# Making h of layer 0 in five turns of 2, 3, 3, 4 and 4 d-tiles, with the adaLN sums of all but the first on VectorE

## The chip, the cores and the metric

The kernel runs on one core of one Trainium2 chip. The metric is the device time of one execution in microseconds; lower is better. Of the kernel before there are three runs, and one further execution that was profiled.

## What is computed

Two layers of a hybrid block over x (256 frames, 2048 channels, float32). The part that matters here is the head of a layer, the conditioned norm (adaLN) and the large input projection:

```python
mod = c_act @ ada_w + ada_b                      # (1, 2048) @ (2048, 6144)
shift, scale, res_gate = jnp.split(mod, 3, axis=-1)
h = rms_norm(x, norm_pre) * (1.0 + scale[:, None, :]) + shift[:, None, :]
proj = h @ w_in                                  # (256, 2048) @ (2048, 14400)
```

Three mixers (retention, a gated recurrence, latent attention) work on slices of `proj`; their outputs are projected, merged by gates, projected again, normed and added to x. Shift and scale of a layer need 2 x 2048 x 2048 weights of `ada_w`, 32 MB, for one row of activations.

## The kernel before

Activations are held with the channels on the 128 partitions, in tiles of 128 channels ("d-tiles"; a layer has 16, `NKT`). Every float32 product is made from split operands: a weight tile is loaded, ScalarE casts it to `wh` (the high part) and VectorE computes `wl = raw - wh` (the rest); then TensorE does three products, xh wh, xh wl, xl wh.

**Loads and splits.** `load_raw` (line 307) issues every load of weights and of adaLN rows on SP, into a ring of four buffers of 1 MB (`rawp`). `load_split` (L331, L332) casts and subtracts in pieces of 1024 columns, into rings of three buffers each (`whp`, `wlp`). A weight tile is 1024 output columns by two d-tiles, 1 MB, in two pieces. The instruction `recent` is the subtraction of the newest tile's first piece.

**Order.** TensorE and SP run in the order in which the code issues their instructions. ScalarE, VectorE and GpSimd are ordered by the framework from priorities (splits 400, closing of sums 300) and dependences; `tc.issue_after(i)` says that what follows comes no earlier than i.

**Turns of layer 0.** Layer 0 starts while no h exists. `KBLOCKS` cuts the 16 d-tiles of h into four blocks of 4. For every block a turn runs over seven groups of 1024 columns of `w_in` (`first`: lx, lg, mqkv, mg, two groups of logits, rq), each with the d-tiles of this block alone: two weight tiles a group, 14 a turn. A group's four PSUM banks (of six in all) are closed after each turn: the first turn's partial sums are copied to SBUF by ScalarE (L473), later ones are added there by VectorE (L475, four adds of 128 x 512 a group). Groups lx, lg, mg and rq hold the weights stationary (`gemm_w`, L416 to L418, 256 columns), the other three the activations (`gemm_x`, L398, 512 columns). In `gemm_x` the steps of the last weight tile of a turn are sorted by halves of the frames.

**The next block, step by step.** While a turn runs, the next block of h is made by a generator, `h_block`. `keep_pace` is called once in each weight tile (in the middle of a tile of two d-tiles) and takes as many steps of the generator as its share of the turn asks: 13 steps (`turns`) over 14 tiles. A step of `ada_strips` loads `nr` rows of `ada_w` per partition (`ada_load`: 512 columns, 4 rows, 1 MB); four loads make the sum for the shift, four that for the scale.

**Two ways to sum.** A sum over 2048 rows has 16 rows on each partition. *Strips*: TensorE multiplies each row (L573) by a matrix of 32 columns, `c_strip`, whose first holds the activation, into one of four strips of 32 partitions of a bank; four strips run side by side. *Adds*: VectorE multiplies a row by the activation and adds it to an accumulator (`ada_add`, L523 for the first, L525 for the others; `issue_after(recent)`), one step after the load. `ON_VECTOR` says which loads go to VectorE: none in the first block, three of four in the others; then eight closing products with `one_strip` (L579) bring the accumulator into the strips' bank. ScalarE copies the bank (L580), TensorE transposes it (L584), VectorE sums over the strips (L587). After both sums `gains` makes the two per-channel factors, and `h_tiles` transposes one or two d-tiles of the normed x (L685), scales them and splits them (L690 or L692, L700, L701).

**Start-up.** The first block has nothing beside it: x, eight adaLN loads and the first weight tiles come in this order, at high priority; half the block's steps go ahead of the first weight load (`early`). Its four d-tiles are scaled on VectorE (L692), later blocks' on ScalarE (L690).

Of the kernel before, what the change touches and what calls it, by code (L numbers as in the profile page):

```python
# [19 lines left out]
P = 128  # L20
# [8 lines left out]
KBLOCKS = [(0, 4), (4, 8), (8, 12), (12, 16)]  # L29
ON_VECTOR = [(), (0, 1, 2), (0, 1, 2), (0, 1, 2)]  # L30
# [25 lines left out]
def hybrid_trunk(ctx: ExitStack, tc: tile.TileContext, a, out):  # L56
# [59 lines left out]
    def mbank():  # L116
        return pm.tile([P, 512], F32, tag="mi", name=nm("mi"))
# [4 lines left out]
    def v3(t, b):  # L122
        return t.rearrange("p (a b) -> p a b", b=b)
# [79 lines left out]
    one_strip = cpool.tile([P, P], F32, name="one_strip")[:, 0:STRIP]  # L203
    nc.gpsimd.memset(one_strip, 0.0)
    nc.gpsimd.memset(one_strip[:, 0:1], 1.0)
# [338 lines left out]
    def ada_strips(l, k0, k1, on_vector):  # L544
# [7 lines left out]
        for which, c0 in enumerate((k0 * P, D + k0 * P)):  # L552
            acc, b = half_slot(ncol), None
            waiting, adds, strips = None, 0, 0

            def add():
                with ExitStack() as order:
                    if recent:
                        order.enter_context(tc.issue_after(recent[-1]))
                    ada_add(acc, waiting, adds == 0)  # L560

            for i, r0 in enumerate(range(0, NKT, nr)):
                rows = ada_load(l, c0, ncol, r0)
                if waiting is not None:
                    add()
                    waiting, adds = None, adds + 1
                if i in on_vector:
                    waiting = rows
                else:
                    b = mbank() if b is None else b  # L570
                    for r, src in rows:
                        j = r % 4 * STRIP
                        mm(b[j:j + STRIP, 0:ncol], c_strip[:, r, :], src, start=strips < 4, stop=not on_vector and r >= NKT - 4, skip_group_check=True)  # L573
                        strips += 1
                yield 1
            if on_vector:
                for i in range(n):
                    j, cs = i * STRIP, slice(i * P, (i + 1) * P)
                    mm(b[j:j + STRIP, cs], one_strip, acc[:, cs], start=False, stop=True, skip_group_check=True)  # L579
            nc.scalar.copy(acc, b[:, 0:ncol])  # L580
# [5 lines left out]
            sums = b[:, 0:ncol].rearrange("p (i j s) -> p i j s", j=4, s=STRIP)[:, :, :, 0]  # L586
# [833 lines left out]
```

## Time and profile before

| | us |
|---|---|
| median of 3 runs (lowest, highest) | 1977.23 (1972.63, 1978.14) |
| profiled execution: its time, its span | 1970.52, 1968.8 |
| PE (TensorE) busy | 1913.3 (97%) |
| VectorE (DVE) busy | 1374.1 (70%) |
| ScalarE (ACT) busy | 963.9 (49%) |
| split's casts, L331 / rests, L332 | 662.3 / 791.4 |

Times in rows are microseconds from the start of the span, busy times are unions of spans, and a mean is in nanoseconds where it says so. PE is TensorE, PEld its weight loads, DVE VectorE, ACT ScalarE, POOL GpSimd, SP the engine that issues the loads. Matmuls overlap, so the distance between starts tells more than a duration. "Idle before" is the time that the engine stood still ahead of an instruction, and behind the arrow stands what ended it.

### The profile page before, as it was taken

What the parts mean: (1) busy time and instruction counts of PE and PEld (TensorE: products, weight loads), DVE (VectorE), ACT (ScalarE), POOL (GpSimd) and SP (SyncE); (2) the same over time, 40 slices, a digit from 0 to 9 for tenths busy, and PEclk for the clock granted to TensorE, in tenths of its full rate; (3) what the DMA queues carried; (4) which work ended last, traced back from release to release, by engine and by line L of the source; (5) the groups of instructions that cost most, each with busy time, mean ns of one, the idle gap of its engine ahead of it and who ended that gap; (6) DMA issues with size and microseconds to landing.
All of it is one profiled execution on the core that took longest, in us unless ns stands there. A gap on an engine that the chain in (4) does not pass through costs nothing.

```text
span 1968.8 us, 25569 instructions
## 1 busy us (share of the span) xinstructions
PE 1913.3 (97%) x10172; PEld 1624.4 (83%) x10172; DVE 1374.1 (70%) x1761; ACT 963.9 (49%) x1252; POOL 104.6 (5%) x89
## 2 busy tenths in 40 slices
PE   4999999989999999999989999999999999999998
PEld 1987989878888888888879888888898888888886
DVE  3668778898877677878766765446675447887565
ACT  3553436934544445444454775444455444544443
POOL 0000000100000010102010010000000001010100
PEclk9999999999999999999999999999999999999999
DMA  9868685468776788888855555555554656877663
GB/s 327 295 219 313 248 304 183 142 234 287 250 268 239 265 271 272 286 284 275 292 205 192 171 171 194 193 190 182 187 185 153 203 192 216 277 283 282 214 214 128
DMA packets 163192, 457.09 MB, mean 232 GB/s; under 512 B 12224, under 2 KB 12240, under 8 KB 163072
## 3 DMA queue, kind: packets, MB, share of 16 engines
q1 hardware_dynamic: 159392, 443.44, 65.4%
q0 software_dynamic: 3536, 11.75, 2.1%
q8 instruction: 79, 1.29, 0.3%
q14 instruction: 41, 0.34, 0.0%
q10 hardware_dynamic: 144, 0.26, 0.0%
HBM read 451.23 MB, written 4.19 MB: 231 GB/s over the span
## 4 chain that ended last, share of the span: by engine, by line
PE 86%; DVE 7%; DMA 4%; ACT 2%; issue 1%; SPq 0%; DVEq 0%; ACTq 0%
PE acc L398 57%; PE acc L432 7%; PE acc L433 4%; PE acc L418 3%; PE acc L417 3%; PE acc L416 3%; DVE wl L332 3%; DMA raw<-in_w_in 2%; DVE slot L525 1%; DMA raw<-in_ada_w 1%; ACT wh L331 1%; PE mi L1003 1%; PE mi L852 1%; PE mi L851 1%; PE mi L573 0%
## 5 line engine op out<-in xcount | busy, mean ns | idle before, releaser
L332 DVE TENSOR_TENSOR wl<-raw,wh 128x1024 fp32r<-128x1024 f32 (+1 forms) x636 | 791.4, 1248 | 488.3 <-ACT wh L331 486.0
L331 ACT CAST wh<-raw 128x1024 fp32r<-128x1024 f32 (+1 forms) x636 | 662.3, 1045 | 826.9 <-PE acc L398 450.4
L398 PE MATMUL acc<-wh,pair 128*128 128x512 f32 x3552 | 991.5, 393 | 2.5 <-ACT wh L331 2.5
L398 PEld LDWEIGHTS acc<-wh,pair 128*128 128x128 f32 x3552 | 660.9, 188 | 146.8 <-issue 9.3
L398 PE MATMUL acc<-wl,pair 128*128 128x512 f32 x1776 | 558.0, 390 | 3.1 <-DVE wl L332 3.1
L398 PEld LDWEIGHTS acc<-wl,pair 128*128 128x128 f32 x1776 | 332.7, 188 | 76.4 <-DVE wl L332 6.6
L525 DVE SCALAR_TENSOR_TENSOR slot<-raw,c_act,slot 128x512 f32<-128x512 f32 x306 | 230.8, 755 | 5.0
L432 PE MATMUL acc<-pair,wh 128*128 128x512 f32 x640 | 228.9, 401 | 0.0
L416 PE MATMUL acc<-pair,wh 128*128 128x256 f32 x640 | 183.3, 286 | 2.4 <-ACT pair L700 1.1
L433 PE MATMUL acc<-pair,wl 128*128 128x256 f32 x640 | 180.5, 282 | 2.7 <-DVE wl L332 2.7
L418 PE MATMUL acc<-pair,wl 128*128 128x256 f32 x640 | 181.5, 284 | 1.4 <-DVE wl L332 1.4
L417 PE MATMUL acc<-pair,wh 128*128 128x256 f32 x640 | 181.4, 283 | 0.5 <-DVE pair L701 0.5
L432 PEld LDWEIGHTS acc<-pair,wh 128*128 128x128 f32 x640 | 120.9, 189 | 28.9
L416 PEld LDWEIGHTS acc<-pair,wh 128*128 128x128 f32 x640 | 123.1, 192 | 3.5 <-ACT pair L700 1.6
L433 PEld LDWEIGHTS acc<-pair,wl 128*128 128x128 f32 x640 | 121.7, 190 | 3.5 <-DVE wl L332 3.3
L418 PEld LDWEIGHTS acc<-pair,wl 128*128 128x128 f32 x640 | 123.0, 192 | 1.8 <-DVE wl L332 1.8
L417 PEld LDWEIGHTS acc<-pair,wh 128*128 128x128 f32 x640 | 123.1, 192 | 1.0 <-DVE pair L701 0.7
L1202 POOL TENSOR_TENSOR slot<-slot,slot 128x512 f32<-128x512 f32 x32 | 51.5, 1625 | 319.5 <-DVE slot L1199 319.5
L475 DVE TENSOR_TENSOR slot<-acc,slot 128x512 f32<-128x512 f32 x84 | 54.0, 685 | 5.6 <-PE acc L418 4.0
L573 PE MATMUL mi<-raw,c_strip 128*32 128x512 f32 x112 | 21.7, 865 | 21.9 <-DMA raw<-in_ada_w 21.9
L1199 DVE TENSOR_TENSOR slot<-acc,slot 128x512 f32<-128x512 f32 x48 | 31.9, 683 | 2.2 <-PE acc L398 2.1
L479 ACT ACTIVATE slot<-acc 128x512 f32<-128x512 f32 x48 | 27.3, 596 | 9.7 <-PE acc L398 8.9
(250 smaller groups left out, 1300.8 us busy)
## 6 DMA issues: line engine op xcount, KB each, us to landing
raw<-in_w_in SPq DMA_DIRECT2D x224, 1024.0 KB, 5.0
raw<-in_ada_w SPq DMA_DIRECT2D x96, 1024.0 KB, 6.8
raw<-in_w_branch SPq DMA_DIRECT2D x48, 1024.0 KB, 6.4
raw<-in_w_out SPq DMA_DIRECT2D x32, 1024.0 KB, 5.5
raw<-in_mla_w_ukv SPq DMA_DIRECT2D x8, 1024.0 KB, 6.4
raw<-in_mla_w_uq SPq DMA_DIRECT2D x8, 768.0 KB, 4.5
slot<-in_x SPq DMA_DIRECT2D x8, 512.0 KB, 8.7
slot<-in_k_decay POOLq DMA_DIRECT2D x4, 512.0 KB, 4.5
```

Source lines behind the costliest of these rows:

```text
L331: nc.scalar.copy(wh, raw[:, c0:c0 + n])
L332: sub = nc.vector.tensor_tensor(out=wl, in0=raw[:, c0:c0 + n], in1=wh.bitcast(F32), op=ALU.subtract)
L398: mm(b[:, 0:w_n], x, ws[:, j * w_n:(j + 1) * w_n], start=st, stop=sp)
L416: mm(dst, wh[:, cs], act.H(kt), start=first, stop=False, skip_group_check=True)
L417: mm(dst, wh[:, cs], act.L(kt), start=False, stop=False, skip_group_check=True)
L418: mm(dst, wl[:, cs], act.H(kt), start=False, stop=last, skip_group_check=True)
L432: mm(v3(b, T), wh[:, cs], act.both(kt), start=kt == 0, stop=False)
L433: mm(b[:, 0:T], wl[:, cs], act.H(kt), start=False, stop=kt == NKT - 1)
L475: nc.vector.tensor_tensor(out=dst, in0=b, in1=dst, op=ALU.add)
L525: nc.vector.scalar_tensor_tensor(acc, src, ada_scalar(r), acc, ALU.mult, ALU.add)
L1199: nc.vector.tensor_tensor(out=gate[hf][:, cs], in0=banks[hf][j], in1=gate[hf][:, cs], op=ALU.mult)
L1202: nc.gpsimd.tensor_tensor(out=dst, in0=dst, in1=gate[hf][:, cs], op=ALU.add)
```

## The change

- `KBLOCKS` is 2, 3, 3, 4 and 4 d-tiles: five turns instead of four. In turns of three d-tiles each group has a weight tile of two d-tiles (1 MB) and one of one (512 KB); the first turn has one tile a group.
- Only the first block is summed by strips. It has 256 columns: two loads of 8 rows a sum, in pieces of 1 KB. `one_strip` and its closing products are gone.
- In all other blocks every load goes to VectorE: 16 adds a sum, of 384 columns in the second and third block (4 rows a load, 768 KB) and of 512 in the fourth and fifth. A load's adds come one step after it, behind the newest tile's first rest. There is no closing product and no copy: the accumulator is transposed as it is and summed over all 128 columns that it then has (the partitions before).
- The pace follows by its formula: 13 steps over 7 tiles in the first turn, 13 over 14 in the others.
- d-tiles from 2 on (before: from 4 on) are scaled on ScalarE, by the condition on `KBLOCKS[1][0]`.

```diff
--- before.py
+++ after.py
@@ -26,8 +26,7 @@
 ROPE = 64
 EPS = 1e-6
 W1 = 1024
-KBLOCKS = [(0, 4), (4, 8), (8, 12), (12, 16)]
-ON_VECTOR = [(), (0, 1, 2), (0, 1, 2), (0, 1, 2)]
+KBLOCKS = [(0, 2), (2, 5), (5, 8), (8, 12), (12, 16)]
 STRIP = 32
 LATE = 800
 ASIDE = [((0, 3),), ((0, 3), (1, 0))]
@@ -200,9 +199,6 @@
     c_strip = cpool.tile([P, NKT, STRIP], F32, name="c_strip")
     nc.gpsimd.memset(c_strip, 0.0)
     nc.vector.tensor_copy(c_strip[:, :, 0], c_act)
-    one_strip = cpool.tile([P, P], F32, name="one_strip")[:, 0:STRIP]
-    nc.gpsimd.memset(one_strip, 0.0)
-    nc.gpsimd.memset(one_strip[:, 0:1], 1.0)
 
     x0 = a["x"].rearrange("b (h p) d -> h p (b d)", p=P)
     out_v = out.rearrange("b (h p) d -> h p (b d)", p=P)
@@ -541,7 +537,7 @@
             use(i, acc)
             release(acc)
 
-    def ada_strips(l, k0, k1, on_vector):
+    def ada_cols(l, k0, k1, strips):
 
 
 
@@ -550,40 +546,33 @@
         nr = 1 << int(math.log2(2048 // ncol))
         cols = small([P, 8], "adac", 2)[:, 0:2 * n]
         for which, c0 in enumerate((k0 * P, D + k0 * P)):
-            acc, b = half_slot(ncol), None
-            waiting, adds, strips = None, 0, 0
-
-            def add():
-                with ExitStack() as order:
-                    if recent:
-                        order.enter_context(tc.issue_after(recent[-1]))
-                    ada_add(acc, waiting, adds == 0)
-
-            for i, r0 in enumerate(range(0, NKT, nr)):
-                rows = ada_load(l, c0, ncol, r0)
-                if waiting is not None:
-                    add()
-                    waiting, adds = None, adds + 1
-                if i in on_vector:
+            acc = half_slot(ncol)
+            if strips:
+                b = mbank()
+                for r0 in range(0, NKT, nr):
+                    for r, src in ada_load(l, c0, ncol, r0):
+                        j = r % 4 * STRIP
+                        mm(b[j:j + STRIP, 0:ncol], c_strip[:, r, :], src, start=r < 4, stop=r >= NKT - 4, skip_group_check=True)
+                    yield 1
+                nc.scalar.copy(acc, b[:, 0:ncol])
+            else:
+                waiting = None
+                for r0 in range(0, NKT + nr, nr):
+                    rows = ada_load(l, c0, ncol, r0) if r0 < NKT else None
+                    if waiting is not None:
+                        with tc.issue_after(recent[-1]):
+                            ada_add(acc, waiting, r0 == nr)
                     waiting = rows
-                else:
-                    b = mbank() if b is None else b
-                    for r, src in rows:
-                        j = r % 4 * STRIP
-                        mm(b[j:j + STRIP, 0:ncol], c_strip[:, r, :], src, start=strips < 4, stop=not on_vector and r >= NKT - 4, skip_group_check=True)
-                        strips += 1
-                yield 1
-            if on_vector:
-                for i in range(n):
-                    j, cs = i * STRIP, slice(i * P, (i + 1) * P)
-                    mm(b[j:j + STRIP, cs], one_strip, acc[:, cs], start=False, stop=True, skip_group_check=True)
-            nc.scalar.copy(acc, b[:, 0:ncol])
+                    if r0 < NKT:
+                        yield 1
             yield 1
             b = mbank()
             for i in range(n):
                 nc.tensor.transpose(b[:, i * P:(i + 1) * P], acc[:, i * P:(i + 1) * P], ident)
             release(acc)
-            sums = b[:, 0:ncol].rearrange("p (i j s) -> p i j s", j=4, s=STRIP)[:, :, :, 0]
+            sums = v3(b[:, 0:ncol], P)
+            if strips:
+                sums = b[:, 0:ncol].rearrange("p (i j s) -> p i j s", j=4, s=STRIP)[:, :, :, 0]
             nc.vector.reduce_sum(out=cols[:, which * n:(which + 1) * n], in_=sums, axis=AX.X)
         gains(l, cols[:, n:2 * n], cols[:, 0:n], k0, k1)
         yield 1
@@ -1105,13 +1094,13 @@
         macc = [[None, None] for _ in range(2)]
         freed = set()
 
-        def h_block(k0, k1, on_vector):
+        def h_block(k0, k1, strips):
             c0 = k0 * P
             while c0 < k1 * P:
                 c1 = min(k1 * P, (c0 // W1 + 1) * W1)
                 normed(xs, xs, r, c0, c1)
                 c0 = c1
-            yield from ada_strips(0, k0, k1, on_vector)
+            yield from ada_cols(0, k0, k1, strips)
             k = k0
             while k < k1:
                 n = 1 if k % 2 else min(2, k1 - k)
@@ -1126,7 +1115,7 @@
                 k0, k1 = KBLOCKS[bi]
                 return 2 * (NKT // (1 << int(math.log2(16 // (k1 - k0)))) + 1) + 1 + (k1 - k0 + 1) // 2
 
-            h0 = start("h0", h_block(*KBLOCKS[0], ON_VECTOR[0]))
+            h0 = start("h0", h_block(*KBLOCKS[0], True))
             last = len(KBLOCKS) - 1
             with tc.high_priority(offset=LATE):
                 for _ in range(turns(0) // 2 + 1):
@@ -1138,7 +1127,7 @@
                 if bi == last:
                     release(*xs[0], *xs[1])
                 else:
-                    ahead = start(f"h{bi + 1}", h_block(*KBLOCKS[bi + 1], ON_VECTOR[bi + 1]))
+                    ahead = start(f"h{bi + 1}", h_block(*KBLOCKS[bi + 1], False))
                     pace[:] = [ahead, turns(bi + 1), len(first) * ((kts[1] - kts[0] + 1) // 2), 0, 0]
                 if bi == last:
                     start("tables", tables())
```

## Rows read from the trace of the kernel before

**Rows 1.** Stages: length, busy (count) of PE, PEld, DVE, ACT, POOL; PEclk, DMA share, GB/s.
```profile
0.00:43.65 43.65, 19.14 (x81) 4.78 (x81) 14.93 (x62) 17.10 (x27) 3.74 (x12) 1.00 0.96 344
43.65:128.60 84.95, 84.48 (x576) 75.21 (x577) 53.00 (x61) 45.76 (x62) 0.57 (x1) 1.00 0.77 273
128.60:216.40 87.80, 85.50 (x578) 74.95 (x578) 72.61 (x103) 37.55 (x47) 0.00 (x0) 1.00 0.75 264
216.40:302.40 86.00, 84.91 (x579) 74.89 (x578) 68.54 (x88) 33.27 (x36) 1.80 (x2) 1.00 0.79 281
302.40:390.80 88.40, 86.91 (x564) 79.17 (x563) 76.11 (x108) 69.46 (x93) 8.43 (x3) 1.00 0.46 151
400.00:450.00 50.00, 44.27 (x211) 36.39 (x210) 48.36 (x60) 18.37 (x22) 2.42 (x1) 0.97 0.66 225
```

**Rows 2.** Chain of work that ended last, start-up: start, duration, what.
```profile
29.36 7.63 DMA raw<-in_ada_w
37.03 1.98 PE mi L573 x8
```

**Rows 3.** Timeline of TensorE: start, duration, instruction, idle before.
```profile
43.65 0.38 PE L416 MATMUL acc<-pair,wh 128*128 128x256 f32 x1 [1.15 <-ACT pair L700]
...
70.35 1.06 PE L573 MATMUL mi<-raw,c_strip 128*32 128x512 f32 x8
71.35 0.73 PE L398 MATMUL acc<-wh,pair 128*128 128x512 f32 x2
...
77.02 0.43 PE L579 MATMUL mi<-slot,one_strip 128*32 128x128 f32 x8
77.38 0.73 PE L398 MATMUL acc<-wh,pair 128*128 128x512 f32 x2
```

**Rows 4.** Turns: who waited (total, times, longest); ScalarE's casts (busy, mean ns).
```profile
ACT wh L331 <- DMA raw<-in_w_in: 47.0, 16, 7.8
...
L331 ACT CAST wh<-raw 128x1024 fp32r<-128x1024 f32 x109 | 113.3, 1048 | 142.9 <-PE acc L417 61.2 <-DMA raw<-in_w_in 47.0 <-PE acc L398 20.4
```

**Rows 5.** Timeline of TensorE in the start-up: strips of two loads, two apart.
```profile
18.27 1.93 PE L573 MATMUL mi<-raw,c_strip 128*32 128x512 f32 x8 [0.68 <-DMA raw<-in_ada_w]
...
23.68 1.93 PE L573 MATMUL mi<-raw,c_strip 128*32 128x512 f32 x8 [0.78 <-DMA raw<-in_ada_w]
```

**Rows 6.** DMA issues of the whole span: count, KB each, median us to landing.
```profile
raw<-in_w_in SPq DMA_DIRECT2D x224, 1024.0 KB, 5.0
...
out<-slot SPq DMA_DIRECT2D x7, 256.0 KB, 2.2
...
raw<-in_w_in SPq DMA_DIRECT2D x4, 256.0 KB, 2.8
```

**Rows 7.** Timeline of VectorE: runs of one operation back to back.
```profile
153.21 2.36 DVE L332 TENSOR_TENSOR wl<-raw,wh 128x1024 fp32r<-128x1024 f32 x2 [0.46 <-ACT wh L331]
...
156.68 3.11 DVE L525 SCALAR_TENSOR_TENSOR slot<-raw,c_act,slot 128x512 f32<-128x512 f32 x4
...
215.49 2.48 DVE L475 TENSOR_TENSOR slot<-acc,slot 128x512 f32<-128x512 f32 x4
```

**Rows 8.** VectorE's groups by form in the turns: count, busy, mean ns, idle before.
```profile
L525 DVE SCALAR_TENSOR_TENSOR slot<-raw,c_act,slot 128x512 f32<-128x512 f32 x69 | 51.7, 750 | 1.3
L994 DVE SCALAR_TENSOR_TENSOR slot<-slot,vec,slot 128x253 f32<-128x253 f32 x8 | 5.8, 733 | 0.0
...
L523 DVE TENSOR_SCALAR slot<-raw,c_act 128x512 f32<-128x512 f32 x7 | 3.4, 481 | 0.0
...
L240 DVE SCALAR_TENSOR_TENSOR slot<-slot 128x320 f32<-128x320 f32 x3 | 1.5, 489 | 0.0
```

**Rows 9.** TensorE's wait behind the turns, and the granted clock (PEclk) around it.
```profile
403.56 0.39 PE L433 MATMUL acc<-pair,wl 128*128 128x256 f32 x1 [2.23 <-DVE wl L332]
...
400.90:404.60 3.70, 1.47 (x9) 1.05 (x8) 3.70 (x3) 2.00 (x2) 1.52 (x1) 1.00 0.29 107
404.60:408.00 3.40, 3.40 (x12) 2.85 (x11) 3.37 (x4) 0.37 (x1) 0.00 (x0) 0.50 0.65 203
```

## The prediction

> **What bounds the kernel now.** I read the busy times by stage first, then the chain of waits, then the timelines of TensorE and VectorE. The stage that the change touches is the making of h in layer 0, from the start to 390.8 us; behind it nothing changes, so what this stage wins or loses is carried to the end.
>
> The stage has a start-up of 43.65 us, in which TensorE works 19.1 us and the DMA engines 96% of the time, and four turns of 84.95, 87.8, 86.0 and 88.4 us, in which TensorE is busy 97 to 99% and the DMA engines 46 to 79% [rows 1]. The start-up hangs on loads: the chain waits 7.6 us for the last adaLN rows, their strips are done at 39.0 us, and 4.6 us later (copy, transposes, sum, gains, h tile, split) the first product starts [rows 2, 3]. In the turns the bound is TensorE's issue rate: 24 matmuls of 512 columns, one weight tile of two d-tiles, take 5.67 us (71.35 to 77.02), so 2.84 us for one group and one d-tile; seven groups make 19.9 us for a d-tile of h [rows 3]. Four of them are 79.5 us; strips (2.7 us a turn, below) and transposes (1.4) bring 83.6, so turns 2 and 3 (87.8 and 86.0) hold some 4 and 2 us of stalls. VectorE is the next bound: 53.0 us in the first turn, 72.6 and 68.5 in the next two [rows 1]. Weights already come late to ScalarE (47 us of its idle time ends on a weight load), which its lead over TensorE still covers [rows 4].
>
> **The start: 12.7 us earlier.** The first block now has two d-tiles: four adaLN loads of 1 MB in place of eight. In the old start-up strips follow each other 2.7 us apart (18.27, then 23.68 two loads later), so that is the time of 1 MB, and the fourth load's strips start at 23.7 and end at 25.7 [rows 5]. With the same 4.6 us behind them the first product would start at 30.3 us, 13.3 us earlier. The pieces of a load become 1 KB (256 columns) instead of 2 KB. No row shows 1 KB. The output's 256 KB in 2 KB pieces land in 2.2 us, 256 KB of the small projection in 256 B pieces in 2.8 us: 0.6 us for 256 KB, so at most 9.6 us for four loads, and 0 at least [rows 6]. 1 KB stands next to 2 KB, so I take 0.6 us. The first weight tile is requested when the first load's strips are done (17.8 us) and its halves are split before 30 us. Gain 12.7 us (3.7 to 13.3).
>
> **Strips leave turns 2 to 4 of the new five: 8.2 us less on TensorE.** In the old first three turns each adaLN sum has 8 strip records of 1.00 us (70.35 to 71.35) and 8 closing ones of 0.36 us (77.02 to 77.38) [rows 3]: 2 sums x 3 turns x 1.36 us. This is on the path, since TensorE is the bound there. Transposes and products stay the same in number.
>
> **VectorE gets more work and less time for it.** An add of 512 columns costs 0.78 us back to back (3.11 / 4), the split's rest 1.18 (2.36 / 2), a partial sum's add from PSUM 0.62 (2.48 / 4) [rows 7]. Before, each of three blocks had 24 adds; now blocks 2 and 3 have 32 of 384 columns, 4 and 5 have 32 of 512. For 384 columns there is no row: 0.49 us at 320, 0.75 at 512, and 0.73 at an odd 253 are its neighbours [rows 8]. I take 0.62 (bounds 0.49 and 0.75). A fifth turn adds 28 PSUM adds (17.4 us). Turn 1 evicts on ScalarE and has none.
>
> The adds of a block cannot spread over the turn: they begin in the pacing call of weight tile 3 and must be done when TensorE comes to the transposes of the second sum, in the call of tile 12. Call one group's share of one d-tile a half. In the turns of three d-tiles (tiles of two halves and of one in alternation) this stretch is 13.5 halves, 13.5 x 2.84 = 38.4 us of TensorE. VectorE can run ahead by the wh and wl buffers, three halves of which one is in use, so 0 to 5.7 us; I take 4, that is 42.4 us. What VectorE has to do in it:
> - turn 2: 13.5 rests (15.9 us), 18 PSUM adds (11.2), 30 adds of 384 at 0.62 and two first ones at 0.4 (19.4), sums and gains 0.7: 47.2 us, 4.8 too much;
> - turn 3: the same with 30 x 0.78 + 2 x 0.48 = 24.4 us: 52.2 us, 9.8 too much;
> - turn 4 (four d-tiles, 18 halves, 51.1 + 4 us): 21.2 + 11.2 + 24.4 + 0.7 = 57.5 us, 2.4 too much.
> The same sum for the old turns (16 halves, 45.4 + 2.7 + 4 = 52.1 us against 47.6) leaves no shortage, where the rows have stalls of 2 to 4 us; those I leave as they are. With a lead of 0 the three shortages are 8.8, 13.8 and 6.4 us, with 5.7 they are 3.1, 8.1 and 0.7. In all 17.0 us (12 to 29; with adds of 0.49 us still 8). That VectorE does not reach full occupancy is seen at 400 to 450 us: 48.4 us busy of 50, and TensorE loses 5.7 us there [rows 1].
>
> **Turn 1: the ring of four load buffers, 8 us.** The first turn has 7 weight tiles (one per group) and 13 steps of the next block, so two steps per tile. SP issues w1 | a0 | w2 a1 a2 | w3 a3 | w4 b0 b1 | w5 b2 b3 | w6 | w7 in this order, and each load waits for the buffer of the fourth before it: w5 for the adds of a3, w6 for those of b1. Adds are ordered behind the first rest of the newest tile. So from the first rest of w5 to that of w6: the other rest 1.18, four adds 2.5, a load 5.0 [rows 6], the cast 1.05 [rows 4], the rest 1.18: 10.9 us, against 5.7 us of products on w5. Less some 1.2 us of lead, w6 is 4 us late. For w5, from the first rest of w3: rests 2.4, eight adds 5.0, then b0 and b1 (0.79 MB each, 4.0 us at 2.7 us a MB) and its own 2.7 us [rows 5], cast and rest 2.2: 16.3 us against two tiles, 11.4; less 2 us of lead, 3 us late. The transposes of the second sum stand in the same pacing call as its last adds: 1 us. In all 8 us; 2 if loads land in 2.8 us as the small ones do, 14 if the leads are gone. Nothing covers it: TensorE has no other work in its order.
>
> **Smaller terms.** In a turn of three d-tiles the last tile is a single one and its pacing call comes behind its products, so the second h tile of the block for turn 3 is transposed at the turn's very end and needed 2.8 us later: 1 us (0 to 2). TensorE waits of 3 us bring a second loss: after a wait of 2.2 us for the weights' rest at 403.56 the granted clock stood at 0.50, that is 1.2 GHz, from 404.6 to 408.0 us [rows 9]. Half of 3.4 us is 1.7 us, and I count it once (0 to 3 times). The Trainium skill, TensorE: Matmul & The Clock Gate, section HAM oscillation, says the same of kernels whose TensorE waits for each tile's load: each such wait is followed by products at half the clock; by that rule both late tiles of turn 1 would pay, 3.4 us instead of 1.7, and the trace has one such dip in the stage's neighbourhood. The 7 us of rope tables that VectorE computes in between move, and cost what they cost now. ScalarE has in turn 1 some 14 casts and 24 copies in about 50 us, and stays off the path.
>
> **The sum.** -12.7 - 8.2 + 17.0 + 8 + 1 + 1.7 = +6.8 us. The profiled execution took 1970.5 us (span 1968.8), so 1977.3 by its measure; the median of the runs is 6.7 us above it, so 1984 us. A difference under 0.3% (5.9 us) is what a measurement of this kernel can't tell from none.
>
> **Rivals.**
> 1. *VectorE nearly keeps pace* (not slower). Adds of 384 columns cost 0.49 us, as the 320 columns of rows 8 do, and VectorE uses the full lead of 5.7 us: the shortage is 8 instead of 17.0, and -2.2 us remain: 1975. It decides where the shortage falls under 10.2 us. For it: the old turns' sum leaves no shortage, and their stalls are small. Against: counted over whole turns, turns 2 and 3 hold 132 us of VectorE work (42 rests, 56 PSUM adds, 64 adds, 4 us of the rest) beside 122 us of products, so about 10 us are lost wherever the lead is, or 6 with the cheap adds. Chance 0.15 alone.
> 2. *The loads run far enough ahead in turn 1* (no change). Of 8 us 2 are left and no clock dip: -0.9 us: 1976. For it: a small load lands in 2.8 us where a large one takes 5.0 [rows 6], and the adds may come in another order; against it: the order of waits through four buffers, which no bandwidth shortens. Chance 0.18 alone.
> 3. *Both* (faster): -12.7 - 8.2 + 8 + 2 + 1 = -9.9 us: 1967. Chance 0.20.
> 4. *Adds stand in front of rests in VectorE's order* (much slower). The code only says that they come no earlier than one rest. A block of four adds (3.1 us) then holds up a split; of 32 blocks, ten that each cost the 2.2 us wait of rows 9 are 22 us more: 2006. For it: nothing else keeps them back; against: the splits have a higher priority, and in the old turns they are not late. Chance 0.08.
>
> **How the numbers follow.** The forecast has 0.39, with an own range of 1978 to 1994. Faster by over 0.3%: rival 3 and a little of 1 and 2, 0.24. Within: the rest of 1 and 2 and the near edge of the forecast, 0.32. Slower: most of the forecast and rival 4, 0.44. The sum's ends are -21.5 + 8 + 2 = -11.5 and -3.7 - 8.2 + 29 + 14 + 2 + 5.1 = +38 us; the outer end needs every bound at once, so the range is 1966 to 1999.
>
> **What would show it.** The first product at about 31 us instead of 43.65. Products in turn 1 lasting 49 to 51 us where 41.5 are work, with TensorE waiting on rests or casts of tiles 5 and 6, and ScalarE waiting on weight loads. VectorE at 95% or more in turns 2 and 3, which take 68 and 74 us where 61 are work (with the stalls that such turns have now). Turn 4 at 85 us; the last turn as now, 88. I am wrong if turns 2 and 3 come out at 64 to 67 us (rival 1), if turn 1 takes under 45 us (rival 2), or if TensorE stops at nearly every tile (rival 4).

## The result and the profile after

The changed kernel takes 2004.82 us (median of 4 runs, 2001.75 to 2008.18), the kernel before 1975.88 (4 runs, 1972.63 to 1978.14) on the same chip: a ratio of 1.0147 [1.0133, 1.0161]. The forecast was 1984 with a range of 1966 to 1999. The direction is right, the size is not: 28.9 us more instead of 6.8.

The profiled execution of the changed kernel took 2008.18 us (span 2006.4), the longest of its four; that of before, 1970.52, is the shortest of its own. So the two profiles stand 37.6 us apart. First the stages of the changed kernel, beside [rows 1]: start-up, the five turns, and all that lies behind (length, busy time and count of PE, PEld, DVE, ACT, POOL; PEclk, DMA share, GB/s).

```profile
0.00:30.96 30.96, 9.96 (x72) 3.97 (x73) 12.67 (x60) 14.98 (x27) 3.66 (x10) 1.00 0.94 307
31.00:86.60 55.60, 47.88 (x276) 41.63 (x276) 38.67 (x54) 30.18 (x45) 0.00 (x0) 0.97 0.75 256
86.60:156.40 69.80, 62.53 (x407) 55.69 (x406) 61.02 (x86) 23.98 (x28) 0.00 (x0) 1.00 0.71 252
156.40:244.50 88.10, 71.44 (x415) 63.10 (x414) 72.82 (x108) 27.72 (x35) 0.57 (x1) 0.88 0.66 227
244.50:332.50 88.00, 82.60 (x550) 74.69 (x549) 75.22 (x96) 33.53 (x37) 1.80 (x2) 1.00 0.78 275
332.50:420.80 88.30, 86.84 (x562) 79.11 (x561) 75.99 (x108) 69.41 (x93) 8.43 (x3) 1.00 0.45 152
420.80:2006.40 1585.60, 1557.29 (x7806) 1318.37 (x7804) 1089.37 (x1343) 761.16 (x989) 90.12 (x71) 0.99 0.66 226
```

The start is 12.7 us shorter, the turns together are 42.7 us longer (389.8 against 347.15), what lies behind is 7.6 us longer (1578.00 before). VectorE is busy 61.0 of 69.8 us in turn 2 and 72.8 of 88.1 in turn 3, 87 and 83%: neither TensorE nor VectorE is full, so waits between the engines set the pace. The waits of TensorE in turns 1 to 4, 31 to 333 us (total, times, longest):

```profile
PE mi L571 <- DVE slot L521: 13.2, 6, 4.4
PE acc L394 <- ACT wh L327: 11.9, 9, 1.9
PE acc L394 <- DVE wl L328: 5.1, 9, 0.8
```

In the four old turns the same view has 1.1 and 1.7 us for the last two lines, and no wait at a transpose. The adaLN transposes (L571) wait for the last add, the products for casts and rests. ScalarE's casts wait for weight loads 88.9 us (24 times), where [rows 4] have 47.0 (16 times). One of the long waits, in turn 3, from the timeline of all engines (start, duration, instruction, idle before):

```profile
188.45 1.53 DVE L521 SCALAR_TENSOR_TENSOR slot<-raw,c_act,slot 128x512 f32<-128x512 f32 x2
188.56 0.34 SPq L303 DMA_DIRECT2D raw<-in_w_in  x1
...
191.75 2.36 DVE L328 TENSOR_TENSOR wl<-raw,wh 128x1024 fp32r<-128x1024 f32 x2 [1.77 <-ACT wh L327]
...
196.13 1.04 ACT L327 CAST wh<-raw 128x1024 fp32r<-128x1024 f32 x1 [3.47 <-DMA raw<-in_w_in]
...
197.21 1.23 DVE L328 TENSOR_TENSOR wl<-raw,wh 128x1024 fp32r<-128x1024 f32 x1 [0.71 <-ACT wh L327]
198.35 0.75 DVE L521 SCALAR_TENSOR_TENSOR slot<-raw,c_act,slot 128x512 f32<-128x512 f32 x1
...
199.41 1.41 DVE L521 SCALAR_TENSOR_TENSOR slot<-raw,c_act,slot 128x512 f32<-128x512 f32 x2
200.21 1.11 PE L571 MATMUL mi<-ident,slot 128*128 128x128 f32 x4 [3.75 <-DVE slot L521]
```

The weight load is issued at 188.56, when a buffer comes free, and lands 7.6 us later. Its cast and its rest follow, and only then the last two adds of the sum (198.35, and the first of two at 199.41). They belong to a load whose first two adds ran at 188.45, so it had landed long before, and VectorE stood still for 1.8 us ahead of 191.75 and 0.7 us ahead of 197.21. But in VectorE's order they stand behind the rest of a tile that had not landed, and TensorE stands still at the transposes. It is not `issue_after(recent)` that puts them there, since it holds the four adds of a load alike. In p1 below, where only the adds' priority is raised above the splits', 0.8 us of the 13.2 us of waits at transposes are left.

The clock, beside [rows 9]: one dip in turn 1 and two of four in turn 3 (columns as in the first view), then, from the timeline of TensorE, the wait ahead of the first one in turn 3 (2.65 us).

```profile
72.40:75.80 3.40, 3.35 (x8) 2.68 (x9) 3.36 (x5) 1.04 (x1) 0.00 (x0) 0.50 0.96 335
...
161.20:164.60 3.40, 3.40 (x19) 3.40 (x18) 2.70 (x8) 0.86 (x1) 0.00 (x0) 0.50 0.29 116
198.70:205.50 6.80, 5.29 (x25) 5.29 (x26) 4.25 (x8) 1.04 (x1) 0.00 (x0) 0.50 0.88 293
```

```profile
159.74 0.39 PE L413 MATMUL acc<-pair,wh 128*128 128x256 f32 x1 [2.65 <-DVE pair L690]
```

PEclk 0.50 is 1.2 GHz. Five such dips (one in turn 1, four in turn 3) hold 23.8 us, and products start at the lower level too (below).

### The profile page after: what moved, and what is told of

Its sections match the earlier page's. It is cut to its first block, busy times and chain, and to the rows that moved or that the text cites. A ratio compares the mean times of both kernels' runs of the same rounds, so it can differ in the third digit from the quotient of the medians.

```text
span 2006.4 us, 25496 instructions
## 1 busy us (share of the span) xinstructions
PE 1918.6 (96%) x10076; PEld 1636.6 (82%) x10076; DVE 1425.8 (71%) x1850; ACT 961.0 (48%) x1250; POOL 104.6 (5%) x87
## 4 chain that ended last, share of the span: by engine, by line
PE 73%; DVE 13%; DMA 8%; ACT 3%; issue 2%; POOL 0%; SPq 0%; ACTq 0%; DVEq 0%
PE acc L394 48%; PE acc L428 6%; DVE wl L328 6%; DMA raw<-in_w_in 5%; PE acc L429 3%; DVE slot L521 3%; PE acc L413 3%; PE acc L414 3%; PE acc L412 3%; ACT wh L327 2%; DMA raw<-in_w_branch 2%; DVE slot L471 1%; DMA raw<-in_w_out 1%; DMA raw<-in_ada_w 1%; PE mi L841 1%
## 5 line engine op out<-in xcount | busy, mean ns | idle before, releaser
L521 DVE SCALAR_TENSOR_TENSOR slot<-raw,c_act,slot 128x512 f32<-128x512 f32 (+1 forms) x360 | 262.4, 731 | 6.1
L412 PE MATMUL acc<-pair,wh 128*128 128x256 f32 x640 | 187.5, 293 | 3.6 <-ACT pair L689 2.0
L413 PE MATMUL acc<-pair,wh 128*128 128x256 f32 x640 | 185.3, 290 | 3.5 <-DVE pair L690 3.5
L414 PE MATMUL acc<-pair,wl 128*128 128x256 f32 x640 | 185.2, 289 | 3.2 <-DVE wl L328 3.2
L429 PE MATMUL acc<-pair,wl 128*128 128x256 f32 x640 | 181.0, 283 | 2.6 <-DVE wl L328 2.6
L428 PEld LDWEIGHTS acc<-pair,wh 128*128 128x128 f32 x640 | 121.6, 190 | 29.1
L412 PEld LDWEIGHTS acc<-pair,wh 128*128 128x128 f32 x640 | 126.9, 198 | 5.3 <-ACT pair L689 2.4
L413 PEld LDWEIGHTS acc<-pair,wh 128*128 128x128 f32 x640 | 126.8, 198 | 4.6 <-DVE pair L690 4.2
L414 PEld LDWEIGHTS acc<-pair,wl 128*128 128x128 f32 x640 | 126.6, 198 | 4.2 <-DVE wl L328 4.2
L429 PEld LDWEIGHTS acc<-pair,wl 128*128 128x128 f32 x640 | 122.5, 191 | 3.4 <-DVE wl L328 3.2
L471 DVE TENSOR_TENSOR slot<-acc,slot 128x512 f32<-128x512 f32 x112 | 72.5, 683 | 13.1 <-PE acc L414 11.3
L1188 DVE TENSOR_TENSOR slot<-acc,slot 128x512 f32<-128x512 f32 x48 | 31.8, 681 | 2.3 <-PE acc L394 2.3
L475 ACT ACTIVATE slot<-acc 128x512 f32<-128x512 f32 x48 | 27.3, 596 | 9.2 <-PE acc L394 8.3
L621 POOL DMA_DIRECT2D slot<-in_norm_post x8 | 4.5, 558 | 489.2 <-DVE wl L328 333.6
```

Source lines behind the costliest of these rows:

```text
L412: mm(dst, wh[:, cs], act.H(kt), start=first, stop=False, skip_group_check=True)
L413: mm(dst, wh[:, cs], act.L(kt), start=False, stop=False, skip_group_check=True)
L414: mm(dst, wl[:, cs], act.H(kt), start=False, stop=last, skip_group_check=True)
L428: mm(v3(b, T), wh[:, cs], act.both(kt), start=kt == 0, stop=False)
L429: mm(b[:, 0:T], wl[:, cs], act.H(kt), start=False, stop=kt == NKT - 1)
L471: nc.vector.tensor_tensor(out=dst, in0=b, in1=dst, op=ALU.add)
```

## Experiments

Ratios are against the kernel before on the same chip, with a 95% interval; times of turns are from each profile. "All adds" stands for the change's second half.

**The two halves.** Five turns with the old sums, and four turns with all adds:

```diff
 # e1: kernel before
-KBLOCKS = [(0, 4), (4, 8), (8, 12), (12, 16)]
+KBLOCKS = [(0, 2), (2, 5), (5, 8), (8, 12), (12, 16)]
-ON_VECTOR = [(), (0, 1, 2), (0, 1, 2), (0, 1, 2)]
+ON_VECTOR = [(), (0, 1, 2), (0, 1, 2), (0, 1, 2), (0, 1, 2)]
 # e2: changed kernel
-KBLOCKS = [(0, 2), (2, 5), (5, 8), (8, 12), (12, 16)]
+KBLOCKS = [(0, 4), (4, 8), (8, 12), (12, 16)]
```

> The kernel before with five blocks of 2, 3, 3, 4, 4 d-tiles alone; the sums stay mixed (three loads of four on VectorE, the fourth as strips on TensorE, in four blocks now). Theory 1 (the added adds on VectorE, and their order there, are the cost): the start's 12.7 us are won, strips cost 2.7 us more than before, turn 1 still loses 10 us or so, turns 2 and 3 are short by some 4 us: 1976 to 1986, turn 3 under 75 us. Theory 2 (the fifth turn is the cost: 28 more PSUM adds and smaller tiles): 1998 or more, turn 3 still over 82 us.

> The changed kernel with the old four blocks of 4: nothing is won at the start, every sum but the first is on VectorE. Theory 1: 8.2 us of strips go, but the adds (32 a block instead of 24) are late in turns 1 to 3, 3 to 6 us each and a clock dip or two: 1980 to 1992. Theory 2: 1968, the strips' 8 us are a gain, since with tiles of two d-tiles the adds have room.

e1: 1987.67 us, 1.0078 [1.0057, 1.0098]; start 31.05, turns 53.0, 69.2, 75.4, 86.3, 88.3. e2: 1978.17, 1.0029 [1.0014, 1.0044]; turns 84.7, 92.4, 87.4, 89.8. Both come out between their two theories. Both halves lose, the five turns more; together they lose more than their sum (0.78 + 0.29 against 1.47%). So the two get in each other's way.

**Is it the adds?** Changed kernel with a quarter of each load's adds (three quarters of the sum left out, loads and order as they are):

```diff
-                            ada_add(acc, waiting, r0 == nr)
+                            ada_add(acc, waiting[:1], r0 == nr)
```

> The changed kernel, with only the first row of each load added on VectorE (three of four adds are left out, so the sums of four blocks are incomplete); loads, waits and order stay. Theory 1: turns 2 to 4 come down to about 63, 63 and 83 us, the clock does not dip in them, and the total is 1960 to 1972. Theory 2: 1990 or more. Theory 3 (the ring of four load buffers and the loads themselves hold up TensorE): turn 1 stays above 50 us and turns 2 and 3 above 68, 1985.

1970.93 us, 0.9989 [0.9979, 0.9998]: 1.6% come back against the changed kernel. Its turns 2 to 4 (columns as above):

```profile
84.90:152.10 67.20, 63.01 (x406) 56.42 (x405) 47.15 (x63) 24.36 (x28) 0.00 (x0) 0.97 0.76 262
152.10:220.80 68.70, 64.66 (x415) 57.21 (x414) 56.03 (x83) 27.77 (x35) 0.57 (x1) 0.98 0.82 291
220.80:301.80 81.00, 81.00 (x551) 75.26 (x550) 58.50 (x72) 33.96 (x37) 1.79 (x2) 1.00 0.86 299
```

Turn 2 gains little, 2.6 us: with VectorE busy only 47 of 67 us it is still 6 us above its products. Adds alone can't be the cause there.

**Is it where the adds and the transposes stand?** e4 puts the transposes one pacing step later (15 steps a turn in place of 13); p1 gives the adds a higher priority than the splits.

```diff
 # e4
-                    if r0 < NKT:
-                        yield 1
+                    yield 1
 # p1
-                        with tc.issue_after(recent[-1]):
+                        with tc.issue_after(recent[-1]), tc.high_priority(offset=500):
```

> The changed kernel with one more step between the last adds of a sum and its transposes on TensorE (15 steps a turn instead of 13); VectorE's work is the same. If TensorE's waits for the adds at the transposes are the cost (14 us of waits in the profile, and the clock dips that follow), 1984 to 1990. If VectorE's throughput is the cost, the wait only moves to the rests of weights: 2000 to 2006.

> The changed kernel, four buffers, the adds with a higher priority than the splits (500 against 400), still not ahead of the newest tile's first rest. If the order on VectorE costs (last adds of a sum stand behind the rest of a later tile, whose load is late), the waits at the transposes shrink and buffers come free earlier: 1988 to 1996. If VectorE's throughput costs: the waits move to the rests, 2002 to 2008.

e4: 1998.01 us, 1.0132 [1.0117, 1.0147]; turns 2 to 4 take 70.2, 78.1, 90.8, the total between its two theories. The waits at the transposes shrink to 0.7 us, and TensorE waits 2.4, 1.6 and 2.0 us for h tiles in their place. p1: 1994.19, 1.0099 [1.0079, 1.0118]; 69.0, 79.0, 87.8. Adds ahead of splits are the better order, not the worse, and neither order brings back more than 10 of the 28.9 us.

**Is it the ring of four?** f1 is the changed kernel with five load buffers; room for it comes from one working slot less (`NSLOT`) and from the strip matrix, which moves into half a slot that is given back after the first block. f3 has the quarter of the adds as well. f0 is the control: the kernel before with five buffers, with g3's edits to its strips (below).

```diff
-NSLOT = 21
+NSLOT = 20
-    rawp = ctx.enter_context(tc.tile_pool(name="rawp", bufs=4))
+    rawp = ctx.enter_context(tc.tile_pool(name="rawp", bufs=5))
-    c_strip = cpool.tile([P, NKT, STRIP], F32, name="c_strip")
+    strip_t = half_slot()
+    c_strip = strip_t.rearrange("p (k s) -> p k s", s=STRIP)
...
+            release(strip_t)
```

> The changed kernel with five load buffers of 1 MB instead of four (one 4 KB slot fewer; the strips' matrix lies in a slot). Theory 3 (the ring of four holds loads back: a load waits for the split or the adds of the fourth before it, and comes too late in turns whose tiles are small): with a fifth buffer TensorE's waits on casts and rests in turns 1 to 3 (some 20 us with their clock dips) go, 1980 to 1988. Theory 1 (adds on VectorE, order and throughput): the waits at the transposes stay, 1998 to 2004.

> The same with five load buffers, and only the first row of each load added (three of four adds left out, as in the quarter run before, which took 1971). Theory 3: without the ring's waits and without the adds the turns take 45, 62, 63, 81 us, so the start's 12.7 us and the strips' 8.2 us come out: 1953 to 1960. If the loads' bandwidth or latency itself is the limit, a fifth buffer changes nothing: 1967 to 1972.

> A control: the kernel before (four turns, mixed sums) with five load buffers and one slot fewer (the strips' matrix in a slot, its last four rows kept aside). If the fifth buffer repairs what the change broke, it does little here, where the turns have 2 to 4 us of waits each: 1966 to 1974. If it is a gain of its own that has nothing to do with the change, 1955 or less, and the gain from a fifth buffer in the changed kernel says nothing about the cause.

f1: 1982.32 us, 1.0033 [1.0023, 1.0043]: four fifths of the loss are gone. f3: 1961.32, 0.993 [0.9913, 0.9947], 1 us above its range. f0: 1994.1, 1.0099 [1.0084, 1.0114], a miss in total. Turns 2 to 4 of f1:

```profile
86.10:153.90 67.80, 62.36 (x406) 56.98 (x405) 60.56 (x87) 24.63 (x28) 0.00 (x0) 0.97 0.76 263
153.90:228.10 74.20, 63.67 (x415) 58.44 (x414) 66.86 (x90) 25.11 (x27) 0.00 (x0) 0.95 0.80 270
228.10:312.70 84.60, 81.38 (x551) 75.17 (x550) 75.00 (x96) 34.06 (x37) 1.49 (x2) 1.00 0.81 280
```

Turn by turn this is the forecast, which had left the ring out of these turns: 68, 74 and 85. Turns 2 to 4 together, in us, where the work of TensorE alone is about 203 (an estimate: ten d-tiles at 19.85 us, three turns of 1.4 us of transposes):

| | all adds | a quarter |
|---|---|---|
| four buffers | 245.9 | 216.9 |
| five buffers | 226.6 | 209.0 |

With five buffers the three quarters of the adds are worth 17.6 us (forecast for all: 17.0), with four 29.0. The control: in the old turns 1 to 3 the fifth buffer gives 2.7 us (256.1 against 258.8); turn 1 is 2.3 us longer, since its products start at the lower clock, and turns 2 and 3 are 4.9 us shorter. f0 nevertheless loses 20 us, in the last turn (95.0 us, with the rope tables in it) and behind it. Its turn 2 and the time behind the stage, then that time in the kernel before and in f1:

```profile
130.20:214.70 84.50, 84.50 (x579) 74.90 (x578) 67.24 (x86) 34.65 (x39) 0.00 (x0) 1.00 0.78 274
...
394.10:1992.80 1598.70, 1577.95 (x7806) 1320.83 (x7804) 1088.38 (x1342) 759.86 (x988) 89.44 (x71) 0.99 0.67 223
...
390.80:1968.80 1578.00, 1552.32 (x7806) 1315.44 (x7804) 1088.90 (x1343) 760.75 (x989) 90.07 (x71) 1.00 0.67 227
...
406.10:1980.40 1574.30, 1553.23 (x7806) 1316.93 (x7804) 1087.69 (x1342) 760.70 (x988) 89.33 (x71) 0.99 0.68 227
```

That turn 2 has no idle TensorE at all. Behind the stage f0 doesn't wait more than the kernel before: TensorE is busy 25.6 us longer with the same 7806 products. It isn't the slot, since f1 has one slot fewer as well and loses nothing there. From 450 to 1950 us the products of 512 columns with `wh` (L398 of the kernel before) have a median record of 393 ns in f0, g2 and g3 and of 389 ns in all other kernels of this document. These three alone also narrow `one_strip` from 128 columns to 32; whether that does it was not tested.

**Five turns, old sums, five buffers.** f1's edits on e1; in g2 the strip matrix keeps its half slot to the last turn, in g3 it is given back after the first block (the last load's strips then use a small copy of four rows).

```diff
 # f0, g2 and g3
-    one_strip = cpool.tile([P, P], F32, name="one_strip")[:, 0:STRIP]
+    one_strip = cpool.tile([P, STRIP], F32, name="one_strip")
 # g2, last turn
-                    release(*xs[0], *xs[1])
+                    release(*xs[0], *xs[1], strip_t)
 # g3, behind the first block
+            release(strip_t)
```

> Five turns with the old mixed sums (1.0078 of before with four buffers) and five load buffers. Theory 3: the waits on casts, rests and loads of turns 1 to 3 (20 us in that profile) mostly go: 1962 to 1972, not slower than before. Theory 2 (the fifth turn's own work): 1980 or more.

> Five turns with the mixed sums and five load buffers again, now with the strips' matrix given back after the first block (in the run before its slot was held through all turns). Theory 3 (the ring): its 15 us of loss become -5 to 0: 1965 to 1976. If it is near 2011 again, the fifth buffer does not help the mixed sums, and the ring is not what costs there.

g2: 2011.09 us, 1.0182 [1.0165, 1.0199]; g3: 2000.34, 1.0133 [1.0112, 1.0155]. A miss in total: both lose some 20 us behind the stage (1598.1 and 1595.2 us, e1 1577.2), as f0 does, with the slower products told above. In the turns the buffer does help: turns 1 to 4 of g3 take 277.0 us, of e1 283.9.

**The tables.** Five buffers also moved the rope tables from turn 3 to the last turn, so f1 against the changed kernel mixes two things. t1 is the changed kernel with the tables right behind the first block, t2 is t1 with five buffers, t3 the kernel before with early tables.

```diff
             h0 = start("h0", h_block(*KBLOCKS[0], True))
 ...
+            start("tables", tables())
+            finish("tables")
 ...
-                if bi == last:
-                    start("tables", tables())
 ...
-            finish("tables")
```

> The changed kernel, four load buffers, with the rope tables' code moved from the last turn to just behind the first block, so that their 7 us of VectorE work fall in the start-up or turn 1 and not in turn 3, where they lay in the profile (160 to 186 us; with five buffers they had moved to the last turn too, so that run did not tell the two apart). If the tables made turn 3 so long (88 us): turn 3 at 74 to 78, 1990 to 1994. If the ring of four buffers did: turn 3 still 84 or more, 1999 to 2006.

> The same with five load buffers (one slot fewer). Beside the run with four, it tells the ring alone. Ring theory: turns 2 to 4 together 12 us or more shorter than with four buffers; tables theory: under 6 us. The last turn is back at 88 us (93 with the tables in it): 1975 to 1979.

> The kernel before with the tables' code moved in the same way. If 7 us of VectorE work cost TensorE only where VectorE is short, turn 2 (87.8 us) comes to 85 or 86 and nothing else moves: 1969 to 1972. If the tables cost as much anywhere: 1973.

t1: 2002.19 us, 1.0142 [1.0125, 1.0159]. t2: 1983.9, 1.0053 [1.0036, 1.007]. t3: 1973.19, 0.9997 [0.9988, 1.0007]. Turn 3 of t1 (80.4 us) lies between its two theories, its total in the range of the ring's; t2 has the gain in its turns that was expected of the ring, and a total above the range. Turns 1 to 4 of t1, then of t2:

```profile
33.20:91.40 58.20, 49.31 (x276) 42.59 (x276) 38.62 (x54) 30.04 (x45) 0.00 (x0) 0.88 0.72 242
91.40:161.70 70.30, 63.94 (x407) 57.20 (x406) 60.91 (x86) 23.95 (x27) 0.00 (x0) 0.98 0.71 250
161.70:242.10 80.40, 68.93 (x414) 61.33 (x413) 66.45 (x89) 24.72 (x27) 0.00 (x0) 0.92 0.72 247
242.10:334.60 92.50, 83.67 (x551) 74.65 (x550) 75.76 (x97) 33.40 (x37) 1.80 (x2) 1.00 0.76 263
```

```profile
33.90:86.00 52.10, 46.43 (x276) 40.16 (x276) 38.66 (x55) 30.01 (x45) 0.00 (x0) 0.97 0.82 272
86.00:153.10 67.10, 62.07 (x407) 57.31 (x406) 60.59 (x87) 24.66 (x27) 0.00 (x0) 0.97 0.77 266
153.10:230.30 77.20, 66.95 (x415) 61.39 (x414) 66.48 (x89) 25.04 (x27) 0.00 (x0) 0.89 0.77 259
230.30:315.30 85.00, 82.85 (x550) 76.60 (x549) 74.77 (x96) 34.06 (x37) 0.91 (x1) 0.98 0.81 278
```

VectorE's and ScalarE's busy times are the same within 1.0 us in each turn; only the ring differs, with the room made for it, and 301.4 us become 281.4: 6.1 less in turn 1, 13.9 in turns 2 to 4. In the two medians 18.3 us. Bandwidth isn't what held t1: with five buffers the DMA share rises in every turn (from 0.71, 0.72 and 0.76 to 0.77, 0.77 and 0.81 in turns 2 to 4). TensorE's waits in turns 2 to 4, first t1, then t2:

```profile
PE acc L394 <- ACT wh L327: 8.7, 7, 3.2
PE mi L571 <- DVE slot L521: 6.3, 3, 2.7
PE acc L413 <- DVE pair L690: 5.9, 3, 2.9
PE acc L394 <- DVE wl L328: 3.8, 7, 0.6
PE acc L414 <- DVE wl L328: 2.0, 4, 0.8
```

```profile
PE mi L572 <- DVE slot L522: 16.8, 5, 7.0
PE acc L414 <- DVE pair L691: 0.3, 1, 0.3
PE acc L413 <- DVE slot L472: 0.3, 1, 0.3
```

The waits for casts and rests of weights are gone; what stays is the wait for the last add of a sum. So the ring of four is shown as a cause, with the tables in one place. The tables themselves are 7.7 us of turn 3 (88.1 to 80.4), but in total moving them gives nothing: the start is 2.2 us later, turns 1 and 4 are longer.

What is left in t2 is the VectorE term. From the first add of a block to the transposes of its second sum VectorE is busy 48.0 of 50.6 us in turn 2 and 54.4 of 57.9 us in turn 3; the forecast had 47.2 and 52.2 us of work. Its 20 us ahead of the transposes at 189.96, which wait 7.0 us, and the changed kernel's stretch ahead of those at 200.21:

```profile
170.00:190.00 20.00, 12.71 (x72) 10.86 (x70) 19.01 (x27) 5.15 (x5) 0.00 (x0) 0.88 0.83 284
```

```profile
176.00:200.20 24.20, 16.78 (x83) 13.18 (x81) 20.80 (x31) 9.22 (x14) 0.00 (x0) 0.90 0.70 234
```

With five buffers VectorE is 95% busy where the sum has its deadline; with four it is 86% busy there, since it waits for loads as well.

**Both orders on top.** f1 with e4's and p1's edits together:

> The changed kernel with five load buffers, transposes one step later, adds before splits: the three measures against the three waits at once. If the causes are the ring and the order of the adds, what is left is VectorE's shortage alone (turns 2 and 3 at 64 and 66 us): 1962 to 1972, not slower than before. If VectorE's throughput was the larger part, the waits come back at the rests: 1980 or more.

1995.8 us, 1.0108 [1.0091, 1.0125]; turns 50.8, 74.2, 78.3, 93.1, 94.8. The waits move to the partial sums' adds (L472: 5.5, 9.0 and 4.9 us in turns 2 to 4). It is 0.75% slower than f1: these two orders, together, don't remove VectorE's shortage.

**The clock at the start.** w1 gives TensorE transposes that nobody reads, behind each load of strips and behind the h tiles:

```diff
+    def warm(n):
+        if not idle:
+            idle.append(bank())
+        for i in range(n):
+            nc.tensor.transpose(idle[0][:, i % 4 * P:(i % 4 + 1) * P], ident, ident)
...
+                    warm(4)   # behind each load of strips
...
+                warm(8)       # behind the first block
```

> The changed kernel with 24 transposes of the identity, into a bank that nobody reads, in TensorE's idle time of the start-up (4 behind the strips of each load, 8 behind the h tiles). The first 7.3 us of products ran at the lower clock in the changed kernel; if that is for want of work before them, they start at the higher one and 3.4 us come back: 2000 to 2002. If not, 2004 to 2006.

1999.88 us, 1.0134 [1.0114, 1.0153]; turn 1 takes 53.4 us instead of 55.6, and its time at the lower clock falls from 10.6 to 6.8 us. The interval overlaps that of the changed kernel, so the gain is not told from none.

**Toward a faster kernel.** Four turns with all adds and early tables (k3: e2 with t1's edit); tables behind the first rest of the second weight tile of turn 1, with 40 of w1's transposes (k5); the same tables with e4's later transposes (k6).

```diff
 # k5 and k6, in place of the start of the tables in the last turn
+                    if bi == 0 and n == first[0]:
+                        with tc.issue_after(recent[-1]):
+                            start("tables", tables())
+                            finish("tables")
```

> Four turns with all sums but the first on VectorE (1.0029 of before) and the tables early. Tables theory: turn 2 (92.4 us, with the tables) comes to 87 as turn 3 has it: 1970 to 1974, not slower than before. Otherwise 1978.

> A version meant to be faster than both: four turns, all sums but the first on VectorE, four load buffers, the rope tables behind the first rest of the second weight tile of turn 1 (in the run before they stood ahead of the first block's tail and made the start 1 us later), and 40 transposes of the identity in the start-up's idle time of TensorE (4 behind each load's strips, 8 at its end). From 1971.7: the start back at 43.7 us or earlier, turn 1 without its 3.4 us at the lower clock: 1966 to 1970, 0.996 to 0.999 of before.

> The same without the warming transposes, with the transposes of the sums one step later (TensorE still waits 2.2 to 2.4 us for the last adds at two places). If VectorE has room in turns of four d-tiles, those waits and their clock dips go: 1963 to 1969. If the delay makes h late at the turn's end (waits for the split of h, as in the five-turn kernel): 1970 to 1976.

k3: 1971.67 us, 0.9992 [0.9982, 1.0001]. k5: 1970.64 against 1973.73, 0.9985 [0.9976, 0.9995] (12 runs against 23). k6: 1974.08, 1.0003 [0.9994, 1.0012]. k5 is the only complete version whose interval lies below 1, by 0.15% in the median, and it has four turns. Since it is the best of several tries, its edge may be less than that or nothing.

## Why the prediction was right and where it was wrong

**Right: the start, turn 1's waits, the last turn.** First product at 30.96 us (forecast 31); the 1 KB pieces cost nothing that shows. Turn 1 waits for casts and rests of tile 5 (at 62.8 and 64.0) and tile 6 (71.2, 72.5) as counted, and for tile 3 as well: 7.3 us in all with the two waits at the transposes, where the term had 8. The turn took 55.6 us all the same, not 49 to 51; 4.2 us of that are the clock (below). So rival 2 falls. The last turn took 88.3 (88). Turn 2 took 69.8 (68), in part by luck: with a quarter of the adds it still takes 67.2, so with four buffers the ring holds it up even without the VectorE shortage that the forecast put there. e1 without the all-adds half already has turn 1 at 53.0, so turn 1's loss is the ring's work, as the term said, and t2 takes 6.1 us of it away.

**Right in size: the VectorE shortage.** The uncertain price, the add of 384 columns, is measured, in VectorE's groups by form in the turns of the changed kernel (beside [rows 8]):

```profile
L521 DVE SCALAR_TENSOR_TENSOR slot<-raw,c_act,slot 128x384 f32<-128x384 f32 x60 | 36.6, 616 | 1.4
...
L519 DVE TENSOR_SCALAR slot<-raw,c_act 128x384 f32<-128x384 f32 x4 | 1.7, 414 | 0.0
```

0.62 and 0.41 us; taken were 0.62 and 0.4. With a fifth buffer TensorE waits for last adds 4.7, 9.9 and 2.2 us in turns 2 to 4 (t2); the forecast had 4.8, 9.8 and 2.4. Rivals 1 and 3 fall with it. Rival 4 falls in its price: p1, which does put adds in front, is faster. That its 2006 us are near the 2004.8 measured is chance.

**The step that failed: "Turn 1: the ring of four load buffers, 8 us".** The ring was counted for turn 1 alone and put at nothing, without a reason, in turns 2 to 4: these were counted as VectorE's throughput alone, with a lead "by the wh and wl buffers". But that lead exists only if the loads are there. A tile of one d-tile holds a whole buffer for half the products (2.84 us), and adaLN loads stand between the tiles. An estimate from the order of issue: with two adaLN loads among them, four buffers hold two or three halves, at most some 8.5 us of products. A load is issued only when VectorE has finished with a buffer, and lands 4.5 to 5.3 us later at the median of turns 1 to 4 (the one above: 7.6). So a late rest delays the next load, which delays the next rest, and the adds wait behind both. The forecast's own mark spoke against it: VectorE was to be 95% busy in turns 2 and 3 and is 87 and 83. The runs put 13.9 us on it in turns 2 to 4 (t1 to t2). The table gives 11.4 us as what ring and adds cost only together (29.0 less 17.6), with the tables in turn 3 in its first row and not in its second.

**Too small: the clock, 1.7 us.** Besides the dips, the products start at the lower level: in the timeline of TensorE they follow each other 0.21 us apart until 38.2 us and 0.12 after.

```profile
37.97 0.41 PE L413 MATMUL acc<-pair,wh 128*128 128x256 f32 x1
38.18 0.33 PE L414 MATMUL acc<-pair,wl 128*128 128x256 f32 x1
38.35 0.28 PE L412 MATMUL acc<-pair,wh 128*128 128x256 f32 x1
38.47 0.28 PE L413 MATMUL acc<-pair,wh 128*128 128x256 f32 x1
```

With the dips, 31 us of the five turns ran at 1.2 GHz. Counted by the products in them that is 11.4 us (4.2 in turn 1, 7.2 in turn 3), where the forecast had one dip. The Trainium skill, TensorE: Matmul & The Clock Gate, section HAM oscillation, describes products at half the clock behind each wait for a tile; the trace agrees for the three longest waits of turns 1 to 4 (2.65, 3.75 and 4.36 us, in turn 3) and for two of the seven between 1.48 and 2.25 us. In turn 1 the two waits at tile 5, 1.48 and 0.53 us, bring no dip, while in turn 3 two waits of 1.49 and 0.53 us (at 180.1 and 181.4) do.

**Taken as free: the tables and what lies behind.** "The 7 us of rope tables ... move, and cost what they cost now": they fell into turn 3, the turn with the least room, and were 7.7 us of it (t1), though the total doesn't show it. "Behind it nothing changes": the work is the same (7806 products), the time in this profile 7.6 us longer, of which 5.1 us are the clock (20.4 us at the lower level against 10.2). Other kernels with 21 slots have 1577 (e1) and 1580 us (e3) there, so no part of it is shown to be the change's.

Together: the turns came out 23 us above the forecast (42.7 against 17.0 + 8 + 1 + 1.7 - 8.2 = 19.5). The ring in turns 2 to 4 is 14 of them and the clock 9.7. The clock isn't part of the ring's 14: by the record t2 spends 27.3 us of turns 1 to 4 at the lower level and t1, but for its start, 23.9.

**Open.** Why the products of f0, g2 and g3 are slower throughout (behind the stage f1 takes 1574 us, f0 1599); why turn 4 of t1 is 4.5 us longer than the changed kernel's; why some waits bring a dip and equal ones don't; what a fifth buffer would be worth without taking a slot, which wasn't tried.

## What to carry to other kernels

Count a ring of load buffers in time of products, not in number: when tiles get smaller or other loads come in between, the same four buffers cover less, and every stage that uses the ring has to be counted, not only the one in which it is seen first. On an engine that works in a fixed order, an add that stands behind the rest of the newest tile inherits that tile's load, even if its own data has landed; a shortage on one engine and a short ring then cost more together than apart. Price a long wait of a nearly full TensorE with the clock behind it: here the five waits that brought a dip, 15.2 us, cost about half as much again. And read a control by its stages: f0's total says nothing about the ring, its turns do.

## What the runs showed of the hardware

In turns 1 to 4 of the changed kernel, three waits of TensorE of 2.65 to 4.36 us each brought 3.4 or 6.8 us at 1.2 GHz; of seven waits of 1.48 to 2.25 us two did, and five did not. After a start-up in which TensorE was busy 10.0 of 31 us, the first 7.2 us of products ran at the lower level, which the PEclk column (1.00) doesn't show; only the spacing does. Adds on VectorE cost 0.62 us for 384 columns and 0.75 to 0.78 for 512. A product of 512 columns had a median record of 393 ns in three kernels and of 389 ns in all others, with PEclk at 0.99 or 1.00 in all of them.
